# Both feed-forward blocks in two phases: all gate and up groups first, then the down projection as seven Strassen block types

## The chip, the cores and the metric

The kernel runs on one core of a Trainium2 chip. Its engines are TensorE (PE; the loading of its stationary operand has a row of its own, PEld), VectorE (DVE), ScalarE (ACT), GpSimd (POOL) and SyncE (SP, which only issues transfers here). Each engine works through its own list of instructions in order, and engines wait for each other by semaphores. The metric is the device time of one launch in microseconds, median over several runs.

## The reference

One decoder layer over 512 tokens of width 1024, in float32: a feed-forward block at half weight, a token mixer, a second feed-forward block at half weight, and a gated per-token embedding.

```python
def swiglu(x, w_gate, w_up, w_down):
    return (jax.nn.silu(x @ w_gate) * (x @ w_up)) @ w_down
...
h = h + 0.5 * swiglu(rmsnorm(h, ffn1_norm[i]), ffn1_w_gate[i], ffn1_w_up[i], ffn1_w_down[i])
n = rmsnorm(h, mix_norm[i])
proj = n @ w_in[i]
...
h = h + jnp.concatenate([ya, yb], axis=-1) @ w_out[i]
h = h + 0.5 * swiglu(rmsnorm(h, ffn2_norm[i]), ffn2_w_gate[i], ffn2_w_up[i], ffn2_w_down[i])
gate = jax.nn.sigmoid(rmsnorm(h, ple_norm[i]) @ ple_w_gate[i] + ple_b_gate[i])
h = h + gate * (p[i] @ ple_w_proj[i])
```

`w_gate` and `w_up` are 1024 x 2816 and `w_down` is 2816 x 1024, in each of the two feed-forward blocks (FFN1 and FFN2 below).

## The kernel before

**Products in three passes.** Every float32 operand is held as a rounded part and a remainder (`hi` and `lo`), and a product is the sum hi·hi + hi·lo + lo·hi on TensorE. A weight tile of 128 x 1024 (512 KB) is loaded (`raw`, `rawb`, `rawd`), cast by ACT into `whi` (L539), and the remainder is taken by DVE into `wlo` (L543). `whi` and `wlo` are rings of three buffers. So the cast for a step can begin only when the step three before it, the last reader of that buffer, has ended on PE. The down steps of the middle of an FFN have `whix` and `wlox`, one buffer each.

**Steps.** The program is a list of steps, each with its load, its cast and split, its product on PE, and work that follows the product (`after`, `post`). One function, `run`, writes all steps out in an order of its own: a step's product goes to PE, and around it the splits of the steps that come next and the `after` work of the steps before. Only `ENTRY`, a table written by hand, overrides that order for the first steps up to well into FFN2. PE, ACT, DVE and SP execute in that order word for word; POOL is ordered by the scheduler.

**Gate and up.** The 2816 features are 22 blocks of 128, taken in pairs: 11 groups per FFN. Group 0 is computed plainly. Groups 1 to 10 use Strassen's scheme in Winograd's form: seven products instead of eight for the 2 x 2 blocks (two halves of the features' rows by two halves of the tokens). Each product is one step of 24 matmuls over 256 columns (L756). They are run as 1, 7, 6, 4, 5, 2, 3. Products 6, 5 and 3 run in the same PSUM bank `a`, one on top of the other, and 4 in `mm`, so the values that stand between are read out on the way:

```python
def gate_sum(self, half):
    ps, kept = ((self.ps["q"], self.u2), (self.ps["a"], self.p7))[half]
    nc.vector.tensor_tensor(self.g[:, :, half], by_half(ps), by_half(kept), ALU.add)
```

`gate_sum(1)` (L896 with `a`) must have read the bank before product 3 writes it again. Around it stand, for each half of the tokens, the multiplication by the norm's factor (L901), the sigmoid on ACT (L903), a product with the factor (L907) and, at the end, the product with the up value (`finish`, L912).

**Down.** When a pair of groups is done, its gated product `g` is split (`ghi` by ACT, L923; `glo` by DVE, L925). Four steps then form its part of the down projection: 24 matmuls over 512 columns each (L255), of two of the eight row blocks of the output. They are not run at once: two of them are taken into each of the following groups.

```python
for i in (1, 7, 2, 6, 4, 5, 3) if j == 1 else (1, 7, 6, 4, 5, 2, 3):
    steps.append(gs[j][i])
    if i in ((5, 3 if at else 4) if j == 1 else (7, 5)):
        steps.append(here.pop(0))
```

So a group is 1, 7, down, 6, 4, 5, down, 2, 3. Each down step's result is added to the residual stream `h` by two DVE instructions (L959).

Of the kernel before, what the change touches and what calls it, by code (L numbers as in the profile page):

```python
# [39 lines left out]
G_6TS = (1, 2, 2, 2, 2, 2)  # L40
HT = T // 2
NP = ND // 2
# [13 lines left out]
product5 after4.1 split7 split7.1 load12 product6 split8:1 sums9 after5:1 split8 after6 after5:2  # L56
split9:2 split10.1:1 after5 product7 split10.1:1 split9 load14 product8 split10.1:1 after7
split10 split10.1 load15 product9 split11 after8 load16 product10 after9 split12 load17 after10
after10.1:1 product11 after11 split13 split14:1 after10.1 split14 product12 after+10 after11.1
after11.2 after12:1 product13 after+11 split15 after13:1 split16 after13:1 after12 product14  # L60
after13 ..after23 split26:1 after23:2 split26 after23 ..split101 after98:1 split101 after98
after+98 load104 product100 cast102 after+98 after99 rest100 split102 load105 split102 load105
product101 cast103 after+99 split103 rest101 load106 product102 cast104 after101 split104
rest102 load107 product103 cast105 after102 after102.1 split105 post102 load108 product104
cast106 after103 after103.1 after103.2 split106 post103 post103.1 load109 product105 cast107
after104 cast108 after104.1 after104.2 split107 split108 split107 post104 load110 product106
cast108 after105 ..product163 product163 split165:1 product163 after162 split165 load170
product164 split166 after163 after163.1 after164:1 product165 after164 product165 after+163
split167 after164 product166 after+164 split168:1 after165 split168 after165 after165.1
after165.2 product167 after+165 split169:1 after167:1 split169 after167:1 split169 after166:1  # L70
split170:1 sums171 split170 after166 split171:1 after166 load174 product168 after+166 split171:1
after+166 after167 split170 sums171 load175 product169 after168
# [11 lines left out]
)  # L84

PAD = {"sb": 96, "ffn_left": 256, "mix_left": 320, "ple_left": 256, "ffn_right": 96, "mix_right": 96, "ple_right": 0}
HEADS = 16
DT_AT = 112  # L90
# [22 lines left out]
def layer_kernel(ctx: ExitStack, tc: tile.TileContext, a: dict, out: bass.AP):  # L113
# [1720 lines left out]
    for side in region:  # L1834
        close_region(side)
# [100 lines left out]
```

## Time and profile before

| what | value |
|---|---|
| time, median of 3 runs | 1040.44 us (1040.24 to 1040.56) |
| profiled execution | 1040.32 us, span 1038.6 us |
| granted TensorE clock, mean | 0.997 |
| busy: PE, DVE, ACT, POOL | 99%, 75%, 50%, 13% of the span |
| matmuls | 6752 |
| DMA queue q1 (issued by SP) | 40304 packets, 128.86 MB, 36.1% of 16 engines' span |
| DMA queue q0 (issued by POOL) | 8640 packets, 31.46 MB, 17.7% |

The span is the time from the first to the last instruction; the profiled execution's own time lies 1.7 us above it. Busy shares are means over stages that differ, and a busy PE says that matmuls follow each other without a gap, not that they are short. The share of a DMA queue is the time that its packets took, as a share of 16 engines over the span. Rows of a timeline read: start in us, duration in us, engine, line, operation, output<-inputs, shapes, number; in brackets the idle time before it and who ended it.

### The profile page before, as it was taken

Reading aid. Unit: us, or ns where it says so; the run is one execution under the profiler, and the core shown is the slowest. Engines: PE = TensorE matmul, PEld = TensorE weight load, DVE = VectorE, ACT = ScalarE, POOL = GpSimd, SP = SyncE. Lnnn points to the kernel's source line nnn. Section 1 sums busy time; section 2 is a strip of 40 time slices with the busy share of each in tenths; the row PEclk is TensorE's granted clock in tenths of the full one; section 3 lists DMA queues with packets and bytes.
Section 4 is the critical chain, followed back from the end, with each engine's and each line's share of the span. In section 5 each row is a group of like instructions: output and inputs, shape, how many; then the busy total and the mean of one; then the engine's idle time right before and its main releaser. Section 6 shows DMA issues by size and latency. Waiting matters only on the chain.

```text
span 1038.6 us, 16733 instructions
## 1 busy us (share of the span) xinstructions
PE 1024.8 (99%) x6752; PEld 943.9 (91%) x6752; DVE 780.9 (75%) x1082; ACT 519.6 (50%) x716; POOL 135.6 (13%) x125
## 2 busy tenths in 40 slices
PE   8999999999999999999999999999999999999996
PEld 7999999999998899888888888899999999999886
DVE  6987776777677787776998757698777767676776
ACT  7754444434444474665854434454444444434554
POOL 0100000000000300044333000111000000000411
PEclk9999999999999999999999999999999999999998
DMA  9997767676623232544532323777767677634412
GB/s 338 320 234 206 204 185 185 167 198 177 145 61 122 71 114 94 158 149 123 159 103 64 119 83 122 223 183 207 206 162 192 160 191 195 191 103 130 135 42 81
DMA packets 50318, 163.55 MB, mean 157 GB/s; under 512 B 5696, under 2 KB 6208, under 8 KB 50240
## 3 DMA queue, kind: packets, MB, share of 16 engines
q1 hardware_dynamic: 40304, 128.86, 36.1%
q0 software_dynamic: 8640, 31.46, 17.7%
q10 hardware_dynamic: 1296, 2.16, 0.7%
q8 instruction: 53, 0.87, 0.3%
q14 instruction: 25, 0.20, 0.1%
HBM read 158.20 MB, written 4.26 MB: 156 GB/s over the span
## 4 chain that ended last, share of the span: by engine, by line
PE 86%; DVE 8%; ACT 2%; issue 2%; DMA 1%; SPq 0%; POOL 0%; DVEq 0%; ACTq 0%; POOLq 0%
PE sm L255 23%; PE mm L756 20%; PE a L756 15%; PE mm L241 6%; PE sm L241 5%; PE mm L255 4%; PE a L241 4%; PE a L255 3%; PE sm L842 1%; DVE wlo L543 1%; PE mm L842 1%; PE a L842 1%; DMA h<-in_x 1%; DVE tmp L1753 1%; PE sm L308 1%
## 5 line engine op out<-in xcount | busy, mean ns | idle before, releaser
L539 ACT CAST whi<-raw 128x1024 fp32r<-128x1024 f32 (+1 forms) x140 | 143.9, 1028 | 133.8 <-issue 42.6
L543 DVE TENSOR_TENSOR wlo<-raw,whi 128x1024 fp32r<-128x1024 f32 (+1 forms) x140 | 172.8, 1235 | 50.0 <-ACT whi L539 49.0
L756 PE MATMUL mm<-xfb,whi 128*128 128x256 f32 x960 | 163.8, 275 | 0.0
L756 PEld LDWEIGHTS mm<-xfb,whi 128*128 128x128 f32 x960 | 147.1, 192 | 1.0
L756 PE MATMUL mm<-xfb,wlo 128*128 128x256 f32 x480 | 132.3, 276 | 0.0
L255 PE MATMUL sm<-ghi,wlox 128*128 128x512 f32 x296 | 112.4, 380 | 0.5 <-DVE wlox L543 0.5
L255 PE MATMUL sm<-ghi,whix 128*128 128x512 f32 x296 | 112.4, 380 | 0.0
L255 PE MATMUL sm<-glo,whix 128*128 128x512 f32 x296 | 112.3, 380 | 0.0
L756 PE MATMUL a<-xfb,whi 128*128 128x256 f32 x640 | 109.2, 275 | 0.0
L756 PEld LDWEIGHTS a<-xfb,whi 128*128 128x128 f32 x640 | 98.7, 192 | 1.1
L756 PEld LDWEIGHTS mm<-xfb,wlo 128*128 128x128 f32 x480 | 92.3, 192 | 0.0
L756 PE MATMUL a<-xfb,wlo 128*128 128x256 f32 x320 | 88.2, 275 | 0.0
L543 DVE TENSOR_TENSOR wlox<-rawd,whix 128x1024 fp32r<-128x1024 f32 (+1 forms) x40 | 46.0, 1150 | 47.5 <-ACT whix L539 47.5
L903 ACT ACTIVATE g<-g 128x512 f32<-128x512 f32 x40 | 25.3, 632 | 106.6 <-DVE g L901 106.6
L543 DVE TENSOR_TENSOR wlo<-rawb,whi 128x1024 fp32r<-128x1024 f32 x52 | 63.6, 1223 | 17.8 <-ACT whi L539 17.7
L771 POOL DMA_DIRECT2D raw<-in_ffn_gu x20 | 17.6, 882 | 393.4 <-DVE h L959 138.1
L241 PE MATMUL sm<-x,whi 128*128 128x512 f32 x224 | 68.5, 388 | 0.0
L539 ACT CAST whi<-rawb 128x1024 fp32r<-128x1024 f32 x52 | 54.3, 1044 | 24.8 <-DVE rawb L766 18.9
L959 DVE SCALAR_TENSOR_TENSOR h<-sm,h 128x512 f32<-128x512 f32 x96 | 62.2, 685 | 3.1 <-PE sm L255 3.1
L255 PEld LDWEIGHTS sm<-ghi,wlox 128*128 128x128 f32 x296 | 56.1, 189 | 8.6 <-DVE wlox L543 0.9
L255 PEld LDWEIGHTS sm<-glo,whix 128*128 128x128 f32 x296 | 56.2, 190 | 6.8
L255 PEld LDWEIGHTS sm<-ghi,whix 128*128 128x128 f32 x296 | 56.2, 190 | 6.8
(388 smaller groups left out, 2394.5 us busy)
## 6 DMA issues: line engine op xcount, KB each, us to landing
raw<-in_ffn_gu SPq DMA_DIRECT2D x56, 512.0 KB, 6.4
rawd<-in_ffn_down SPq DMA_DIRECT2D x40, 512.0 KB, 4.2
rawb<-in_ffn_gu SPq DMA_DIRECT2D x32, 512.0 KB, 5.4
raw<-in_ffn_gu POOLq DMA_DIRECT2D x30, 512.0 KB, 5.7
raw<-in_w_in SPq DMA_DIRECT2D x28, 512.0 KB, 3.7
s<-in_ffn_gu SPq DMA_DIRECT2D x20, 512.0 KB, 7.3
s<-in_ffn_gu POOLq DMA_DIRECT2D x20, 512.0 KB, 8.6
raw<-in_w_out SPq DMA_DIRECT2D x16, 512.0 KB, 3.5
```

Source lines behind the costliest of these rows:

```text
L241: nc.tensor.matmul(ps, w, turned(x), start=first and n == 0, stop=last and n == 2, skip_group_check=True)
L255: nc.tensor.matmul(ps[:, tok], wt[:, c], turned(xt[:, tok]), start=first and k == i == 0, stop=last and k == len(xs) - 1 and i == len(by_p ...
L308: nc.tensor.matmul(ps[:, c : c + 1], part[:, c * P : (c + 1) * P], ones[:, 0:1], start=part is t, stop=part is not t or more is None,)
L539: nc.scalar.copy(self.hi[:, c], self.raw[:, c])
L543: nc.vector.tensor_tensor(self.lo[:, c], self.raw[:, c], self.hi[:, c].bitcast(F32), ALU.subtract)
L756: nc.tensor.matmul(o, wt[:, c], turned(xt), start=fresh and p == m == n == 0, stop=last and n == 2, skip_group_check=True,)
L771: nc.gpsimd.dma_start(w21.raw, self.src[0], accum_op=ALU.add)
L842: nc.tensor.matmul(ps, (whi, whi, wlo)[n][:, c], t[:, 0:2, n % 2].rearrange("p s (b i) -> p s i b", b=2), start=not lower and p == n == 0, ...
L903: nc.scalar.activation(t, t, AF.Silu)
L959: nc.vector.scalar_tensor_tensor(two(h[d]), back(ps[d]), 0.5, two(h[d]), ALU.mult, ALU.add)
L1753: engine.tensor_tensor(t, t, emb[d][:, tok], ALU.mult)
```

## The change

Each FFN becomes two phases. All ten Strassen groups run back to back; their gated products stay in one tile `G` of 128 x 2 x 2 x 10 x 256. Group 0's down projection follows as four plain steps of 12 matmuls over 512 columns. The down projection of the ten other groups is then one Strassen-Winograd product over 2 x 2 blocks: seven products, each of five steps of 24 matmuls over 256 columns, in the order 1, 7, 6, 4, 5, 2, 3.

```diff
+        steps = groups[0].plain_steps(at)
+        for j in range(1, NJ + 1):
+            steps += [gs[j][i] for i in ((1, 7, 2, 6, 4, 5, 3) if groups[j].turned else (1, 7, 6, 4, 5, 2, 3))]
+        steps += [down(i) for i in range(ND // 2)]
+        steps += blocks_down(a[f"{name}_dw"], shared, steps[-4:], out_norm, after, closed)
...
-            mine = groups[g0 - n : g0]
-            pending = [down(part, mine, i, each, last) for i in range(ND // each)]
-        steps += pending
```

The sums of weight blocks are formed by the DMA queue of POOL, which adds a block from memory to a tile that is already on chip. The sums of feature blocks are formed by DVE in `G` (`form`), and each of the seven feature operands is split in two parts by ACT and DVE (`split_form`) while the product before it runs. `ends` gives the work behind the last step of a product.

```diff
+            elif i in (4, 5, 2):
...
+                nc.sync.dma_start(raw, dw[{4: 3, 5: 2, 2: 1}[i], t])
+                if i == 5:
+                    nc.gpsimd.dma_start(raw, dw[3, t], accum_op=ALU.add)
...
+        def form(i, part):
...
+            nc.vector.scalar_tensor_tensor(to, one, -1.0, other, ALU.mult, ALU.subtract)
+
+        def split_form(i, part):
...
+            nc.scalar.copy(hi, g)
+            yield
+            nc.vector.tensor_tensor(lo, g, hi.bitcast(F32), ALU.subtract)
...
+        def q_done():
+            yield from add_to(2, 0, ps["q"], ALU.subtract)
+            yield from add_to(2, 0, kept["u2"], ALU.subtract, True)
+
+        ends = {
+            1: seeds, 7: lambda: keep("p7", "raw0", ps["q"]), 6: lambda: keep("u2", "g", ps["a"]),
+            4: q_done, 5: lower_done, 2: lambda: add_to(0, 0, ps["x"], ALU.add), 3: upper_done,
+        }
...
+            def split():
+                yield from w.split_by_engine(chain[t] if i in (1, 7, 6, 3) else kept[i, t])
+                if i in (1, 7, 6):
+                    yield
+                    nc.gpsimd.dma_start(chain[t], dw[{1: 2, 7: 3, 6: 1}[i], t], accum_op=ALU.add)
...
+            if i in (6, 4, 5):
+                also(at[0], "post", lambda i=i: form(i, parts[0]))
+                also(at[1], "post", lambda i=i: form(i, parts[1]))
+            also(at[0], "post", lambda i=i: split_form(i, parts[0]))
+            also(at[2], "post", lambda i=i: split_form(i, parts[1]))
```

```diff
-product5 after4.1 split7 split7.1 load12 product6 split8:1 sums9 after5:1 split8 after6 after5:2
+product5 after4.1 split7 split7.1 product6 split8:1 sums9 after5:1 split8 after6 after5:2
...
-+after166 after167 split170 sums171 load175 product169 after168
```

**What moves on DVE in a gate-and-up group.** Before, from the split for the down step behind product 5 to the additions of that step (line numbers of the kernel before; `wlo_1229` is the remainder for product 2, `wlo_1264` for product 3, `wlo_1296` for the next group's product 1, `g` the gated product):

```order
L543 TENSOR_TENSOR wlox_1199<-rawd_1029,whix_1198 128x1024
L543 TENSOR_TENSOR wlo_1229<-rawb_1067,whi_1228 128x1024
L896 TENSOR_TENSOR g_1232<-mm_1069,u_202_1196 128x2x256
L901 SCALAR_TENSOR_TENSOR g_1232<-g_1232,rall_497 128x2x256
L907 TENSOR_TENSOR g_1232<-g_1232,rall_497 128x2x256
L543 TENSOR_TENSOR wlo_1264<-rawb_843,whi_1263 128x1024
L896 TENSOR_TENSOR g_1232<-a_146_757,p_156_837 128x2x256
L901 SCALAR_TENSOR_TENSOR g_1232<-g_1232,rall_497 128x2x256
L907 TENSOR_TENSOR g_1232<-g_1232,rall_497 128x2x256
L543 TENSOR_TENSOR wlo_1296<-raw_196_1132,whi_1295 128x1024
L959 SCALAR_TENSOR_TENSOR h_96<-sm_1236,h_96 128x512
L959 SCALAR_TENSOR_TENSOR h_100<-sm_1249,h_100 128x512
```

Now the same place reads as follows (L519 is the remainder, L874 `gate_sum`, L879 and L885 the two multiplications, L890 `finish`; `wlo_1517` is for product 2, `wlo_1545` for product 3, `wlo_1577` and `wlo_1611` for the next group's products 1 and 7):

```order
L519 TENSOR_TENSOR wlo_1517<-rawb_1354,whi_1516 128x1024
L519 TENSOR_TENSOR wlo_1545<-rawb_1191,whi_1544 128x1024
L874 TENSOR_TENSOR G_629<-mm_1422,u_211_1514 128x2x256
L879 SCALAR_TENSOR_TENSOR G_629<-G_629,rall_488 128x2x256
L885 SCALAR_TENSOR_TENSOR G_629<-G_629,rall_488 128x2x256
L519 TENSOR_TENSOR wlo_1577<-raw_201_1420,whi_1576 128x1024
L874 TENSOR_TENSOR G_629<-a_197_1387,p_208_1484 128x2x256
L879 SCALAR_TENSOR_TENSOR G_629<-G_629,rall_488 128x2x256
L885 SCALAR_TENSOR_TENSOR G_629<-G_629,rall_488 128x2x256
L519 TENSOR_TENSOR wlo_1611<-raw_1452,whi_1610 128x1024
```

The chain of the gate now stands one remainder later: the one for product 3 is ahead of both sums, and the one for the next group's first product is between them.

**What moves on DVE in the down projection.** Before, a down step costs DVE the remainder of its weights, two additions to `h` and, once for four of them, the remainder of the gated product (the first rows of this piece, `glo`; the rows between belong to the next group):

```order
L543 TENSOR_TENSOR wlox_1058<-rawd_913,whix_1057 128x1024
L925 TENSOR_TENSOR glo_1062<-g_943,ghi_1061 128x1024
L766 TENSOR_TENSOR rawb_843<-rawb_843,s_163_878 128x1024
L543 TENSOR_TENSOR wlo_1096<-rawb_843,whi_1095 128x1024
L543 TENSOR_TENSOR wlo_1129<-raw_881,whi_1128 128x1024
L543 TENSOR_TENSOR wlo_1159<-s_163_878,whi_1158 128x1024
L959 SCALAR_TENSOR_TENSOR h_95<-sm_1100,h_95 128x512
L959 SCALAR_TENSOR_TENSOR h_99<-sm_1113,h_99 128x512
```

Now, between the splits for product 4's last steps and those for product 5's third (L994 is `form`, L1004 the remainder of a feature operand `xfb`, L1028 and L1026 are `q_done`; `wlo_3433` belongs to product 4's last step, `wlo_3465`, `wlo_3494` and `wlo_3528` to product 5's first three):

```order
L519 TENSOR_TENSOR wlo_3433<-xfa_3048,whi_3432 128x1024
L994 SCALAR_TENSOR_TENSOR G_629<-G_629 128x1024
L1004 TENSOR_TENSOR xfb_3437<-G_629,xfb_3437 128x1024
L519 TENSOR_TENSOR wlo_3465<-xfa_3113,whi_3464 128x1024
L994 SCALAR_TENSOR_TENSOR G_629<-G_629 128x1536
L519 TENSOR_TENSOR wlo_3494<-xfa_3113,whi_3493 128x1024
L1004 TENSOR_TENSOR xfb_3437<-G_629,xfb_3437 128x1536
L1028 TENSOR_TENSOR h_96<-h_96,sm_3015 128x2x256
L1028 TENSOR_TENSOR h_97<-h_97,sm_3016 128x2x256
L1026 TENSOR_TENSOR h_96<-h_96,g_3370 128x2x256
L1026 TENSOR_TENSOR h_97<-h_97,g_3370 128x2x256
L519 TENSOR_TENSOR wlo_3528<-raw_3179,whi_3527 128x1024
```

Forms, remainders of features and the additions of the product before stand in one queue with the remainders of the weights.

**What moves on PE at the end of FFN1.** Before, the norm's sums (L308, with `ssum` from POOL) stand behind two whole units of the mixer (the end of the second):

```order
L241 MATMUL mm_3669<-x_3656,whi_3600 128x512
L241 MATMUL mm_3669<-x_3657,whi_3600 128x512
L241 MATMUL mm_3669<-x_3656,wlo_3601 128x512
L308 MATMUL sm_3704<-ones_77,ssum_3551 128x1 [waits PE_49,Pool_49]
L308 MATMUL sm_3704<-ones_77,ssum_3551 128x1 x3
L241 MATMUL sm_3711<-x_3512,whi_3647 128x512 [waits PE_49]
```

Now they stand (L284) behind three halves of 12 matmuls, and ahead of the third unit:

```order
L217 MATMUL mm_3988<-x_4018,whi_3945 128x512 [waits Activation_49]
L217 MATMUL mm_3988<-x_4019,whi_3945 128x512 [waits DVE_49]
L217 MATMUL mm_3988<-x_4018,wlo_3946 128x512
L284 MATMUL sm_4066<-ones_76,ssum_3809 128x1 [waits Pool_49]
L284 MATMUL sm_4066<-ones_76,ssum_3809 128x1 x3
L217 MATMUL sm_4073<-x_3801,whi_4001 128x512
```

The wait for POOL has moved up by 12 matmuls over 512 columns.

353 lines of the change are left out of this document (217 added, 136 removed).

## The prediction

> **What bounds the kernel now.** I read the page's first lines, then the chain that ended last inside one gate-and-up group of FFN1, then what DVE and ACT did in that group, then the DMA queues.
>
> ```profile
> span 1038.6 us, 16733 instructions
> PE 1024.8 (99%) x6752; PEld 943.9 (91%) x6752; DVE 780.9 (75%) x1082; ACT 519.6 (50%) x716; POOL 135.6 (13%) x125
> ...
> q1 hardware_dynamic: 40304, 128.86, 36.1%
> q0 software_dynamic: 8640, 31.46, 17.7%
> ```
>
> PE is without work for 13.8 us of the span (1038.6 - 1024.8). So the kernel gains only from fewer or shorter matmuls, and loses whatever time another engine makes PE wait. In the chain, each line is one step: start, length, bank, line, matmuls.
>
> ```profile
> 185.06 2.68 PE a L756 x24
> 187.74 2.68 PE mm L756 x24
> 190.42 2.68 PE a L756 x24
> 193.10 5.18 PE sm L255 x24
> 198.28 2.68 PE mm L756 x24
> 200.96 2.68 PE a L756 x24
> 203.64 2.46 PE mm L756 x22
> ```
>
> These are product 6, 4, 5, a down step, 2, 3 and the next group's 1. Each begins where the one before ends. A step of 24 matmuls over 256 columns takes 2.68 us, one over 512 takes 5.18.
>
> DVE in the same stretch, with the remainder for product 2, `gate_sum(0)`, its two multiplications, the remainder for product 3, `gate_sum(1)`:
>
> ```profile
> 190.54 1.22 DVE L543 TENSOR_TENSOR wlo<-rawb,whi 128x1024 fp32r<-128x1024 f32 x1
> 191.67 0.69 DVE L896 TENSOR_TENSOR g<-mm,u 128x512 f32<-128x512 f32 x1
> 192.39 0.69 DVE L901 SCALAR_TENSOR_TENSOR g<-g,rall 128x512 f32<-128x512 f32 x1
> 193.78 0.69 DVE L907 TENSOR_TENSOR g<-g,rall 128x512 f32<-128x512 f32 x1 [0.69 <-ACT g L903]
> 194.72 1.22 DVE L543 TENSOR_TENSOR wlo<-raw,whi 128x1024 fp32r<-128x1024 f32 x1 [0.25 <-ACT whi L539]
> 195.86 0.68 DVE L896 TENSOR_TENSOR g<-a,p 128x512 f32<-128x512 f32 x1
> ```
>
> From the start of the first remainder to the end of `gate_sum(1)` it is 196.54 - 190.54 = 6.00 us. `gate_sum(1)` reads bank `a`, which product 3 writes from 200.96: there are 4.42 us to spare. They are there because a down step of 5.18 us stands between.
>
> **The change, part by part.** *Fewer matmul columns.* Per FFN 20 down steps of 5.18 us (103.6) become 35 of 2.68 (93.8); group 0's four steps stay. That is -9.8 us per FFN, -19.6 in all. The gate and up products do not change in number.
>
> *The gate's chain without its cover.* `whi` has three buffers, so the cast for product 3 waits until product 4 has ended, which is when product 5 starts; call that moment zero. That the ring binds like this stands in one row of ACT: a cast beginning as the step at 198.28 ends (200.96).
>
> ```profile
> 200.93 1.05 ACT L539 CAST whi<-raw 128x1024 fp32r<-128x1024 f32 x1 [2.05 <-issue]
> ```
>
> In the new order the remainder for product 3 stands ahead of `gate_sum(0)`, so the same six DVE instructions as in the rows above, with the remainders one step later, begin at 1.05 and `gate_sum(1)` ends at 1.05 + 6.00 = 7.05. Product 3 is due after products 5 and 2, at 5.36. PE waits 1.7 us. Behind it the queue has room: two multiplications and the sigmoid between them end near 9.3, the next group's second remainder at 10.5, due at 12.4. So it is one wait of 1.7 per group, each group anew. Check from the other side: 4.42 to spare, less the 5.18 removed, less some 1.0 that the first remainder starts later: -1.8. Nine groups of an FFN at 1.7, and the last at about 0.9, since the next step's remainder has 512 columns instead of 1024: 16.2 per FFN, +32.4 in all. Bounds: 0 if something lets the cast start a step earlier, 2.4 per group if the semaphores between the three engines add more than in the rows.
>
> *DVE in the block products.* Durations, the page's first two rows of DVE, then the groups kept apart by shape, then one sum of two weight blocks from the timeline:
>
> ```profile
> L543 DVE TENSOR_TENSOR wlo<-raw,whi 128x1024 fp32r<-128x1024 f32 (+1 forms) x140 | 172.8, 1235 | 50.0 <-ACT whi L539 49.0
> ...
> L959 DVE SCALAR_TENSOR_TENSOR h<-sm,h 128x512 f32<-128x512 f32 x96 | 62.2, 685 | 3.1 <-PE sm L255 3.1
> ```
>
> ```profile
> L925 DVE TENSOR_TENSOR glo<-g,ghi 128x1024 fp32r<-128x1024 f32 x20 | 27.4, 1372 | 21.9 <-ACT ghi L923 21.9
> L923 ACT CAST ghi<-g 128x1024 fp32r<-128x1024 f32 x20 | 27.3, 1364 | 46.1 <-DVE g L912 44.6 <-DVE g L874 1.5
> ```
>
> ```profile
> 208.24 1.24 DVE L766 TENSOR_TENSOR rawb<-rawb,s 128x1024 f32<-128x1024 f32 x1
> ```
>
> From the remainder for product 4's third step to that for product 5's third, DVE has five weight remainders (6.17), two forms (1.24, and 1.86 for the one with 1536 columns, scaled), two feature remainders (1.37 and 2.06, scaled) and the four additions of `q_done` (2.74): 15.4. It also waits for ACT's copy behind each form: 1.36, and 2.05 less the remainder that stands between, 0.8. That makes 17.6. Neighbours in the rows overlap by 0.09 (190.54 + 1.22 against 191.67); for eleven that is -1.0, so 16.6. PE does five steps in 13.4. It waits 3.2 us. Products 6 and 4 have forms but not these additions: 16.6 - 2.4 = 14.2, 0.8 each. Products 1 and 3 have additions, and 3 the mixer's operands, in place of forms: I take 0.8 each, as for those with forms; products 7 and 2 fit. 6.4 per FFN, +12.8 in all. Bounds: 0 (if the queue has run ahead) and 20.
>
> *The hand-over to the mixer and to the last gate.* The last product ends only `h`'s upper row blocks. Behind it come two additions, the squares on ACT and four sums on POOL, and PE asks for them after three halves of 12 matmuls, 3 x 2.59 = 7.8 us.
>
> ```profile
> 338.28 6.48 POOL L298 TENSOR_TENSOR ssum<-ssum,tmp 128x512 f32<-128x512 f32 x4 [5.75 <-ACT tmp L297]
> ```
>
> Four sums take 6.5 us; with one addition and the operands and squares on ACT ahead of them (some 3.5 us) that is 10.0, a wait of 2.2. Twice: +4.4, bounds 0 and 6. The order written by hand ends early now, and the start of FFN2 and of the mixer run in `run`'s own: I take +3, with 0 and 8 as bounds (8 is over half of all the time that PE was idle before).
>
> *Transfers.* Nothing is added to PE's path if they keep ahead. The loads of q1 take 36.1% of 1038.6 us for 128.86 MB, 1.53 us for 512 KB; those of q0 17.7% for 60 of 512 KB, 3.06 us each. A group has five of the one and three of the other: 16.8 us, of a period of 18.8 + 1.7. The down phase has 20 plain ones and 20 that add: 91.8 us, of 93.8 + 10.4 + 6.4 = 110.6 us. That fits, but POOL issues the adding ones in one queue, behind tiles that must come free first: +2, bounds 0 and 16.
>
> *Without cost:* the gains of 0.5 ride on instructions that were there; ACT is at 50%; `L894` is one DVE instruction of 0.69 in every second group and runs after `gate_sum(1)`.
>
> The sum: -19.6 + 32.4 + 12.8 + 4.4 + 3 + 2 = +35.0 on the profiled 1040.32, 1075.3. That execution is 0.12 us below the median, so I give 1075.
>
> **A rule beside it.** One group of before, with its down steps, reads: length, then busy time of PE, PEld, DVE, ACT, POOL, and the granted clock.
>
> ```profile
> 185.10:214.20 29.10, 29.10 (x218) 27.83 (x217) 20.92 (x24) 12.91 (x15) 2.54 (x3) 1.00 0.69 178
> ```
>
> DVE is busy 72% of it. Without two down remainders, four additions and `glo` 14.3 us are left of 18.8, 76%; in the block products it is 12.7 of 13.4 (five remainders, forms and feature remainders), 95%. The Trainium skill ("Perfetto Trace Analysis", Optimization Strategy) says that where the most contended engine changes between regimes of a kernel, interleaving them may help. It gives no figure; spread evenly, DVE's work would fit under PE's, and the sum would be the -19.6 alone. By that rule the change, which takes the two regimes apart, gives up cover, and these rows agree.
>
> **The rivals.** *The waits stay hidden, and it is faster.* For it speaks that no row of before shows PE waiting in a group; against it, the order of DVE and the ring. It decides at `gate_sum(1)` ending before 5.36; below 0.6 us of wait per group and none in the block products the change gains. Then 1040.4 - 19.6 + 3 = 1024.
>
> *Only the gate's wait is real.* DVE may run ahead in the down phase, since the steps of 5 us are gone and nothing else is queued. 1040.4 - 19.6 + 32.4 = 1053.
>
> *Transfers become the bound.* A group at present has the DMA engines busy for 0.69 of its time, without waiting. If adding transfers can't be had at more than 0.69 of 16 engines, the down phase takes 91.8 / 0.69 = 133 us in place of 110.6 and a group 24.3 in place of 20.5; half of that, since loads run ahead into the plain steps, is 11 + 19 per FFN, over 1100; with the down phase alone, 1075 + 22 = 1097.
>
> *The clock drops.* It is 1.00 in the row above and lower only at the end, where PE is idle:
>
> ```profile
> 1030.00:1038.60 8.60, 1.11 (x8) 0.87 (x8) 3.26 (x10) 2.16 (x4) 0.00 (x0) 0.69 0.57 213
> ```
>
> My longest wait is 3.2 us, twice. If it halved the clock for some 4 us afterwards, that would be +2 each, 1079. The Trainium skill ("TensorE: Matmul & The Clock Gate", HAM oscillation) warns of idle gaps above about 3.4 us; no row of before has such a gap between matmuls.
>
> **How the numbers follow.** Both waits, as summed: 0.65, from 1060 to 1090. Only the gate's wait: 0.12. Transfers: 0.09. The clock: 0.02. Hidden waits and a gain: 0.09. Within the 0.2% that a measurement can tell here: 0.03, where parts of each cancel. The point is the likeliest case's, 1075. The range leaves out the gain, the draw, and the worst of the transfers: 1050 to 1094. Faster 0.09, same 0.03, slower 0.88.
>
> **What would show it.** In the profile after: matmuls 7472 in place of 6752; a step of product 3 in every group starting about 1.7 us behind the end of product 2, with DVE's sum of `a` as the releaser; in the down phase one gap of about 3 us at product 5's third step; the sums of POOL as a wait of some 2 us behind both FFNs; the clock at 1.00. Gaps released by DMA would mean the third rival. I'm wrong if the group's period is 18.8 us: then the chain of DVE started earlier than the ring allows by my reading.

## The result: 1137 us, 9% slower, and the profile after

The changed kernel takes 1137.25 us (1135.79 to 1139.86, 4 runs), 1.0935 times the kernel before (interval 1.0915 to 1.0956). The forecast was 1075, with a range up to 1094: the sign was right, the size was not. The profiled execution took 1137.24 us. Its page, in the lines that answer to those of before, then the mean granted clock:

```profile
span 1135.5 us, 18390 instructions
PE 1039.8 (92%) x7472; PEld 973.3 (86%) x7472; DVE 827.8 (73%) x1084; ACT 576.9 (51%) x764; POOL 169.4 (15%) x165
```

```profile
core 0: 1135.5 us, clock 0.976
```

Two things stand in the page's second line. PE is without work for 95.7 us (1135.5 - 1039.8), where it was 13.8 before: 81.9 more. And PE is busy 15.0 us longer, though its work by 2.68 and 5.18 us a step is 19.6 us shorter: its matmuls took 34.6 us longer than that. Most of it is the clock: its mean fell from 0.997 to 0.976, which is 24 us of such a span.

Where it went, by stage. Of before, then of after: FFN1 from the first product of group 1, the mixer, FFN2, the last gate (length, busy PE, PEld, DVE, ACT, POOL, granted clock, DMA share, GB/s).

```profile
39.10:341.70 302.60, 302.10 (x2209) 287.57 (x2208) 226.77 (x259) 143.43 (x174) 28.52 (x31) 1.00 0.65 175
341.70:653.90 312.20, 311.95 (x1755) 273.59 (x1754) 243.77 (x399) 167.92 (x272) 58.14 (x40) 1.00 0.36 112
653.90:979.70 325.80, 324.83 (x2318) 307.31 (x2317) 241.13 (x290) 150.61 (x184) 33.49 (x35) 1.00 0.66 179
979.70:1038.60 58.90, 50.13 (x323) 45.25 (x321) 38.55 (x82) 30.02 (x47) 12.39 (x11) 0.95 0.19 65
```

```profile
39.40:387.00 347.60, 309.17 (x2569) 302.54 (x2568) 249.23 (x259) 169.48 (x194) 45.26 (x51) 0.97 0.71 181
387.00:706.20 319.20, 315.15 (x1756) 275.35 (x1755) 244.19 (x400) 170.32 (x276) 61.15 (x42) 0.99 0.38 118
706.20:1073.40 367.20, 328.16 (x2678) 319.08 (x2677) 263.11 (x289) 177.04 (x203) 45.83 (x51) 0.98 0.69 175
1073.40:1135.50 62.10, 51.46 (x324) 46.52 (x322) 40.51 (x85) 32.70 (x51) 14.12 (x12) 0.94 0.30 102
```

FFN1 is 45.0 us longer, FFN2 41.4, the mixer 7.0, the last gate 3.2, the start 0.3. In FFN1 the gate and up groups and the down projection part here:

```profile
39.40:264.30 224.90, 199.44 (x1682) 197.41 (x1680) 153.04 (x171) 101.49 (x127) 23.87 (x28) 0.95 0.69 178
264.30:387.00 122.70, 109.72 (x890) 105.12 (x889) 96.18 (x89) 67.99 (x68) 21.39 (x23) 0.99 0.74 188
```

The 70 products of the groups should take 70 x 2.68 = 187.6 and took 224.9: 37.3 more. The down projection should take 10.4 + 93.8 = 104.2 and took 122.7: 18.5 more. FFN2 loses 35.2 and 17.8. The waits of PE, in the list of the trace: engine, bank and line that wait, who was waited for, us in all, times, the longest.

```profile
PE a L731 <- DVE G L874: 47.4, 19, 4.6
PE a L1091 <- DVE wlo L519: 14.2, 10, 2.9
PE sm L231 <- DVE h L930: 8.5, 6, 1.6
```

Half of the idle time stands in the first line: product 3 waits for `gate_sum(1)` (L874), as forecast, but not evenly. In FFN1 every second group looks as forecast. DVE, with the remainder for product 3 and the two sums, and PE's first matmul of product 3:

```profile
119.42 1.23 DVE L519 TENSOR_TENSOR wlo<-raw,whi 128x1024 fp32r<-128x1024 f32 x1 [0.80 <-ACT whi L515]
120.56 0.68 DVE L874 TENSOR_TENSOR G<-mm,u 128x512 f32<-128x512 f32 x1
...
124.75 0.68 DVE L874 TENSOR_TENSOR G<-a,p 128x512 f32<-128x512 f32 x1
```

```profile
125.58 0.46 PE L731 MATMUL a<-xfb,whi 128*128 128x256 f32 x2 [1.80 <-DVE G L874]
```

Moment zero, product 5's first matmul, is 118.25; the remainder starts at 1.17, `gate_sum(1)` ends at 7.18 and product 3 starts at 7.33: due at 5.36, it is 1.97 late. (The timeline shows 1.80, since the modelled end of the last matmul lies 0.17 behind the next step's due start. Waits below are as the timeline shows them.) In the group behind it, POOL, ACT and PE:

```profile
127.06 0.84 POOL L746 DMA_DIRECT2D raw<-in_ffn_gu  x1 [15.76 <-DMA raw<-in_ffn_gu]
128.81 0.86 POOL L749 DMA_DIRECT2D s<-in_ffn_gu  x1 [0.91 <-DMA s<-in_ffn_gu]
133.54 0.85 POOL L783 DMA_DIRECT2D rawb<-in_ffn_gu  x1 [3.87 <-DVE wlo L519]
```

```profile
141.34 1.05 ACT L515 CAST whi<-rawb 128x1024 fp32r<-128x1024 f32 x1 [3.18 <-DMA rawb<-in_ffn_gu]
```

```profile
148.57 0.64 PE L731 MATMUL a<-xfb,whi 128*128 128x256 f32 x2 [3.99 <-DVE G L874]
```

L783 is the adding transfer that forms product 3's weights. POOL issues it behind the two sums for the next group (L746, L749); it lands 7.8 us after its issue, and the cast starts at 141.34 where moment zero was 139.05. Those 2.3 us pass down the whole chain: 3.99 in place of 1.80. And behind the long wait the matmuls are slow. The 24 matmuls of product 3 after 1.80 us of wait, after 3.99, and after the 2.27 at 103.15:

```profile
125.58:128.40 2.82, 2.82 (x25) 2.82 (x26) 1.85 (x3) 1.60 (x2) 0.84 (x1) 1.00 0.37 145
148.57:152.90 4.33, 4.33 (x24) 4.33 (x25) 3.39 (x4) 1.56 (x2) 0.00 (x0) 0.61 0.94 183
103.15:107.50 4.35, 4.35 (x25) 4.35 (x26) 3.41 (x4) 1.57 (x2) 0.85 (x1) 0.64 0.96 159
```

So the late transfer costs such a group 2.2 us of wait and 1.5 of clock.

In the down projection, the forecast wait at product 5's third step is there: DVE's four additions of `q_done` and the remainder, then PE, with 2.88 us where 3.2 was forecast. Not forecast were waits in group 0's plain steps: PE stands until DVE has emptied the bank `sm` into `h` (the first PE row below).

```profile
342.90 1.26 DVE L1028 TENSOR_TENSOR h<-h,sm 128x512 f32<-128x512 f32 x2
344.09 1.27 DVE L1026 TENSOR_TENSOR h<-h,g 128x512 f32<-128x512 f32 x2
345.30 3.48 DVE L519 TENSOR_TENSOR wlo<-raw,whi 128x1024 fp32r<-128x1024 f32 x3
```

```profile
274.80 0.67 PE L231 MATMUL sm<-xfa,whi 128*128 128x512 f32 x2 [1.58 <-DVE h L930]
...
346.56 0.49 PE L1091 MATMUL a<-xfb,wlo 128*128 128x256 f32 x1 [2.88 <-DVE wlo L519]
```

At the hand-over to the mixer PE waits 3.81 us for four sums of POOL that took 7.44 (forecast 2.2, for 6.5):

```profile
391.28 7.44 POOL L274 TENSOR_TENSOR ssum<-ssum,tmp 128x512 f32<-128x512 f32 x4 [10.64 <-ACT tmp L273]
```

### The profile page after: what moved, and what is told of

It reads as the page before. It is cut to its first block, busy times and chain, and to the rows that moved or that the text cites. A ratio compares the mean times of both kernels' runs of the same rounds, so it can differ in the third digit from the quotient of the medians.

```text
span 1135.5 us, 18390 instructions
## 1 busy us (share of the span) xinstructions
PE 1039.8 (92%) x7472; PEld 973.3 (86%) x7472; DVE 827.8 (73%) x1084; ACT 576.9 (51%) x764; POOL 169.4 (15%) x165
## 5 line engine op out<-in xcount | busy, mean ns | idle before, releaser
L519 DVE TENSOR_TENSOR wlo<-raw,whi 128x1024 fp32r<-128x1024 f32 (+3 forms) x162 | 195.3, 1208 | 58.6 <-ACT whi L515 58.5
L515 ACT CAST whi<-raw 128x1024 fp32r<-128x1024 f32 (+3 forms) x162 | 163.2, 1011 | 135.7 <-PE a L217 24.0
L731 PE MATMUL a<-xfb,whi 128*128 128x256 f32 x640 | 126.2, 301 | 49.8 <-DVE G L874 47.4
L731 PEld LDWEIGHTS a<-xfb,whi 128*128 128x128 f32 x640 | 109.3, 214 | 53.0 <-issue 50.5
L519 DVE TENSOR_TENSOR wlo<-rawb,whi 128x1024 fp32r<-128x1024 f32 x76 | 93.5, 1231 | 71.2 <-ACT whi L515 70.9
L731 PE MATMUL a<-xfb,wlo 128*128 128x256 f32 x320 | 95.3, 298 | 0.8 <-DVE wlo L519 0.8
L1091 PE MATMUL a<-xfb,whi 128*128 128x256 f32 x480 | 84.1, 280 | 1.3 <-ACT whi L515 1.2
L1091 PE MATMUL a<-xfb,wlo 128*128 128x256 f32 x240 | 68.1, 284 | 14.2 <-DVE wlo L519 14.2
L1091 PEld LDWEIGHTS a<-xfb,whi 128*128 128x128 f32 x480 | 74.2, 195 | 2.7 <-ACT whi L515 2.2
L519 DVE TENSOR_TENSOR wlo<-s,whi 128x1024 fp32r<-128x1024 f32 x36 | 45.8, 1282 | 33.1 <-ACT whi L515 32.9
L731 PEld LDWEIGHTS a<-xfb,wlo 128*128 128x128 f32 x320 | 68.7, 215 | 1.0 <-DVE wlo L519 1.0
L746 POOL DMA_DIRECT2D raw<-in_ffn_gu x20 | 17.3, 864 | 338.2 <-DMA raw<-in_ffn_gu 115.3
L1002 ACT CAST xfb<-G 128x1024 fp32r<-128x1024 f32 (+1 forms) x28 | 46.0, 1641 | 29.8 <-DVE G L994 29.8
L1091 PEld LDWEIGHTS a<-xfb,wlo 128*128 128x128 f32 x240 | 46.7, 195 | 16.2 <-DVE wlo L519 16.1
L1004 DVE TENSOR_TENSOR xfb<-G,xfb 128x1024 fp32r<-128x1024 f32 (+1 forms) x28 | 46.4, 1656 | 18.0 <-ACT xfb L1002 17.9
```

What stands on the lines that cost most here:

```text
L515: nc.scalar.copy(self.hi[:, c], self.raw[:, c])
L519: nc.vector.tensor_tensor(self.lo[:, c], self.raw[:, c], self.hi[:, c].bitcast(F32), ALU.subtract)
L731: nc.tensor.matmul(o, wt[:, c], turned(xt), start=fresh and p == m == n == 0, stop=last and n == 2, skip_group_check=True,)
L746: nc.gpsimd.dma_start(w21.raw, self.src[0], accum_op=ALU.add)
L1002: nc.scalar.copy(hi, g)
L1004: nc.vector.tensor_tensor(lo, g, hi.bitcast(F32), ALU.subtract)
```

## The experiments

The theory after the comparison: (A) the cover of the down steps is gone, which costs 1.97 us per group; (B) the late sum for product 3 adds to that in every second group; (C) waits of about 2 us and more lower the clock behind them; (D) the order that `run` writes causes most of the down projection's loss. Rivals: transfers as such are the bound, or DVE's total work is. Ratios are to the kernel before.

### 1. The gate's chain first

```diff
-... split, after, i in (1, 7, 6, 3))
+... split, after, i in (1, 7, 6, 4, 5, 3))
```

The last argument says that the `after` work of the step goes ahead of the next splits.

> The kernel after, with products 4 and 5 of a gate-and-up group marked urgent, so that their gate sums stand ahead of the next remainder on DVE; not an instruction more or less. Theory A (place of the gate chain behind product 3's remainder, whose cast waits for a weight sum that lands late in every second group, and the clock loss that long waits bring): the waits ahead of product 3, 2.0 us in one group and 2.4 to 4.7 in the next, fall to 0.2 to 0.5 in all, the slow product 3 behind them goes, 1137 becomes 1065 to 1085. Rival B (the DMA engines are full in this phase): the transfers are the same, so the period of a group of about 22 us stays and the time is above 1120.

Measured: 1123.69 us, 1.0802 (1.0784 to 1.082). The gain is 13.6 us, well short of the 52 to 72 expected. The waits for the gate's sum are 21.8 us where they were 47.4, and the even groups wait some 0.4 us; the odd ones still wait, because now the late remainder stands in DVE's queue ahead of the second multiplication and `gate_sum(1)`:

```profile
97.55 0.69 DVE L879 SCALAR_TENSOR_TENSOR G<-G,rall 128x512 f32<-128x512 f32 x1
100.75 1.23 DVE L519 TENSOR_TENSOR wlo<-rawb,whi 128x1024 fp32r<-128x1024 f32 x1 [2.51 <-ACT whi L515]
101.89 0.69 DVE L885 SCALAR_TENSOR_TENSOR G<-G,rall 128x512 f32<-128x512 f32 x1
102.49 0.69 DVE L874 TENSOR_TENSOR G<-a,p 128x512 f32<-128x512 f32 x1
```

An in-order queue passes a late transfer on to whatever stands behind it. That pointed at (B) as a cause of its own.

### 2. Without the late sum

```diff
-                if i == 6:
-                    yield
-                    nc.gpsimd.dma_start(w11.raw, self.src[1], accum_op=ALU.add)
```

> The kernel after, without the adding transfer that forms product 3's weights behind product 6 (product 3 multiplies product 6's weights; one of eight 512 KB transfers of a group is left out). Theory A: the groups with 2.4 to 4.7 us come down to the 2.0 of the others and no product 3 runs slow, -17 us per FFN: 1100 to 1108. Rival B (full DMA engines): a gain of an eighth or more in every group alike, also in those with 2.0. A third one (the clock alone makes the difference between the groups): nothing changes, 1130 to 1138.

Measured: 1107.40 us, 1.0643 (1.0628 to 1.0659), 29.9 us less than the changed kernel. The list of waits has product 3's as follows (L871 is `gate_sum`):

```profile
PE a L731 <- DVE G L871: 34.2, 20, 2.6
```

34.2 in 20 waits is 1.71 each; PE is busy 1027.4 us in place of 1039.8. So (B) and what follows it in the clock are 29.9 us, and (A) is left at about 2 us per group. The groups alone gain more: those of both FFNs, by the profiles, take 415.3 us (38.95 to 246.03 and 711.60 to 919.85) where the changed kernel takes 447.7, so 32.4 of their 72.5 us of loss go and 40.1 stay.

### 3. The cover taken away in the kernel before

The second down step of groups 4 to 9 of FFN1 stands behind product 3 instead of behind product 5; nothing else differs.

```diff
-if i in ((5, 3 if at else 4) if j == 1 else (7, 5)):
+if i in ((5, 3 if at else 4) if j == 1 else (7, 3) if name == "ffn1" and 4 <= j <= 9 else (7, 5)):
```

> The kernel before, with the second down step of groups 4 to 9 of FFN1 taken from behind product 5 to behind product 3; the same steps. Theory A: without a step between product 5 and product 2, these six groups each wait 1.9 us or more ahead of product 3, and those whose weight sum is late 2.4 or more with a slow product behind: +11 to +25 us, 1052 to 1065. Rival C (the down steps protect by lending DVE and DMA time to the group as a whole, wherever they stand): within 3 us of 1040.

Measured: 1053.13 us, 1.012 (1.0104 to 1.0135), 12.6 us more than before.

```profile
PE a L756 <- DVE g L896: 10.8, 6, 1.8
```

Six waits of 1.80, as in the changed kernel, and 2.1 us of time for each. The work of every engine is the same as before: it is the place of the down step that hid the chain, and (A) is shown. No sum is late here, though POOL's order is as in the changed kernel.

### 4. Group 0's down steps

Experiment 1, and the additions of the plain down steps ahead of the next splits.

```diff
-                lambda: w.split_by_engine(), (add,),
+                lambda: w.split_by_engine(), (add,), True,
```

> As e1_gate_first, and group 0's four down steps marked urgent as well, so that their additions to h stand ahead of the next remainder on DVE. Theory A: the waits of 0.7 to 1.6 us of those steps for a PSUM bank, 5.0 us per FFN, fall to under 2: 7 to 10 us less than e1_gate_first. If instead they come from the late weights of these steps, the two are the same within 2 us.

Measured: 1121.27 us (1113.95 to 1125.2), 1.0766 (1.0725 to 1.0808). The waits for `h` fall from 11.7 to 2.8 us, but the times of the two kernels overlap: by time alone this is inconclusive.

### 5. Product 3 behind the next group's product 1

```diff
+            if j > 2:
+                at3 = steps.index(gs[j - 1][3])
+                steps[at3], steps[at3 + 1] = steps[at3 + 1], steps[at3]
```

> The kernel after, with product 3 of groups 2 to 9 run behind the next group's product 1 instead of ahead of it: the same instructions, and one step of 2.68 us more between product 5 and product 3. Theory A (gate sum of bank a and the late weight sum are both due at product 3, at 5.36 us, and ready at 7.2 and later): due at 8.04, both are met in time, the waits of eight groups in each FFN and their slow products go, about 28 to 32 us per FFN: 1137 becomes 1072 to 1085. Rival B (transfers fill the phase): under 15 us gained. Rival D (only the place moves: product 3 waits less, but the next group's first products wait instead, since DVE's queue is the bound): 20 to 40 us gained, with waits at product 7 or 6.

Measured: 1113.98 us, 1.0705 (1.0687 to 1.0723). The even groups wait no more; the odd ones that were moved still wait 2.06 to 2.81 us in FFN1 and 1.06 to 2.53 in FFN2, since the sum now lands later too. POOL, then ACT:

```profile
129.71 0.86 POOL L749 DMA_DIRECT2D s<-in_ffn_gu  x1 [1.01 <-DMA s<-in_ffn_gu]
130.25 1.18 POOL L783 DMA_DIRECT2D rawb<-in_ffn_gu  x1
```

```profile
143.22 1.04 ACT L515 CAST whi<-rawb 128x1024 fp32r<-128x1024 f32 x1 [3.58 <-DMA rawb<-in_ffn_gu]
```

It was issued right behind two others and took 13.0 us to the cast. More time for the chain does not help when the transfer's place in the queue sets its end.

### 6. The same, and the down projection's additions in a better order

Experiment 5 with the edit of experiment 4, and `q_done` and `lower_done` behind the next splits.

```diff
-            s = Step(product, ..., (ends[i],) if last else (), last)
+            s = Step(product, ..., (ends[i],) if last else (), last and i not in (4, 5))
```

> As e5_third_later, and two places in the down phase: group 0's four plain steps urgent (additions to h ahead of the next remainder on DVE), and the additions behind products 4 and 5 not urgent (behind the next remainder). Expected against e5_third_later: the plain steps lose some 4 us of their 5.6 per FFN, as e1 and e4 showed in waits (11.7 against 2.8 us for both FFNs); product 5's third step waits about 0.5 us in place of 2.9, with the slow matmuls behind it gone: 10 to 16 us less in all, 1058 to 1072. If product 5's wait is one for the adding transfers, it stays and only the plain steps gain.

Measured: 1101.81 us, 1.0599 (1.0583 to 1.0615), 12.2 us less than experiment 5. The difference is as expected, the time is not, since the odd groups still waited. In the profiled executions 9.2 us of the difference lie in the down projections (245.0 to 235.8 us for both), 6.7 of them in the plain steps. So (D) is shown for about 9 of the 36.3 us that they lose.

### 7. More matmuls

Product 2's 24 matmuls are issued twice in each group: 480 more, 53.6 us of PE's time by 2.68 each.

```diff
                 self.product(i, to, fresh)
+                if i == 2:
+                    self.product(i, to, fresh)
```

> The kernel after, with the 24 matmuls of product 2 issued twice in every Strassen group (the up value of one half of the tokens counts that product twice): 480 matmuls, 53.6 us of PE work more. Theory A with the clock (the waits ahead of product 3 are idle time, and those of 2.4 us and more also slow the matmuls behind them): the filler falls into the waits, the slow products go; 1125 to 1140, no slower than without it. Theory A without a cost of the clock: +4 to +10 us, 1141 to 1148. Rival (PE or its feed is the bound in this phase): +54 us, 1190.

Measured: 1128.72 us, 1.084 (1.0812 to 1.0868): 8.5 us faster than the changed kernel, with 480 more matmuls.

```profile
PE a L731 <- DVE G L876: 4.9, 7, 1.2
```

The waits for the gate's sum go from 47.4 to 4.9 us. By the clock, 0.987 of 1126.0 in place of 0.976 of 1135.5, some 12.6 us more come back. A group is bound by the length of its chain, not by PE's work. This run alone doesn't speak against DVE, whose work is what it was (828.2 us); experiment 14 does, where the same work takes 87.6 us less.

### 8. POOL in the program's order

POOL is added to the engines whose instructions the scheduler may not reorder; L783 then stands ahead of the next group's two sums.

```diff
     ORDERED = {
-        mybir.EngineType.PE, mybir.EngineType.Activation, mybir.EngineType.DVE, mybir.EngineType.SP
+        mybir.EngineType.PE, mybir.EngineType.Activation, mybir.EngineType.DVE, mybir.EngineType.SP, mybir.EngineType.Pool
     }
```

> The kernel after, with POOL's instructions in the order in which the program names them, as the other four engines have it: the adding transfer for product 3's weights then stands ahead of the two for the next group, not behind them. Theory A' (in every second group that transfer lands late because POOL's queue serves the next group's two sums first): all waits ahead of product 3 become 2.0 us and the slow products go, as without the transfer: 1100 to 1112. Rival (it lands late because the DMA engines are full, in whatever order): within 8 us of 1137.

Measured: 1111.05 us (1105.98 to 1115.95), 1.0682 (1.0636 to 1.0728), 26.2 us less. POOL at the same group:

```profile
128.23 0.84 POOL L783 DMA_DIRECT2D rawb<-in_ffn_gu  x1 [19.18 <-DVE wlo L519]
128.77 1.19 POOL L746 DMA_DIRECT2D raw<-in_ffn_gu  x1
129.30 1.53 POOL L749 DMA_DIRECT2D s<-in_ffn_gu  x1
```

All transfers are there, and most of what experiment 2 gained by leaving one out is gained by its place in the queue: 26.2 of 29.9 us in the time, 23.9 of 32.4 in the groups. Transfers as such are not the bound of the groups.

### 9 and 10. Both orders, then sums asked for earlier

Experiment 9 is experiment 6 with the edit of 8.

> e6_later_and_order with POOL in program order. Theory A': the 2.0 to 2.8 us that every second group still waits ahead of product 3 there (19.2 us in the waits, and some 6 us of slow matmuls) go, since the sum now lands before its new due time: 1068 to 1082. Rival as above: 1095 or more.

Measured: 1074.77 us, 1.0327 (1.03 to 1.0355), 27.0 us less than experiment 6. Product 3's waits for the sum are 6.2 us in 4. With the cover back and the sum in time, (A) and (B) are nearly gone. Experiment 10 asks for the weight sums a step earlier, and for the norm's sums 12 matmuls later:

```diff
-                    do(i + 3, "sums")
...
+            do(i + 4, "sums")
...
-    behind_product(2, mix_steps[1].late, mix_steps[2].late)
+    behind_product(2, lambda: mix.update(ps=mix_norm.sums()), mix_steps[1].late, mix_steps[2].late)
```

> e9_order_all, with the sum of product 6's weights one step earlier on DVE, and the norm's sums for the mixer asked for by PE 12 matmuls (2.6 us) later. Expected: the 0.4 and 0.6 us that a group waits at products 7 and 6 (about 1 us in 16 groups) go or halve, and the 3.8 us behind FFN1 become 1.2, with its slow matmuls: 8 to 18 us less than e9_order_all. If the sum's own weights are not there a step earlier, nothing is gained in the groups.

Measured: 1060.84 us, 1.0202 (1.0175 to 1.0229), 13.9 us less than experiment 9.

### 11. Sums on POOL instead of adding transfers

For product 5's weights in the down projection; besides, product 2's additions stand behind the next splits, and the mixer's operands are formed a step later.

```diff
-                    nc.gpsimd.dma_start(raw, dw[3, t], accum_op=ALU.add)
+                    nc.gpsimd.tensor_tensor(raw, raw, kept[4, t], ALU.add)
...
-            s = Step(product, ..., last and i not in (4, 5))
+            s = Step(product, ..., last and i not in (2, 4, 5))
...
-        also(made[2][3], "post", lambda: lower_parts((4, 5)))
-        also(made[2][4], "post", lambda: lower_parts((6, 7)))
+        also(made[2][4], "post", lambda: lower_parts((4, 5)))
+        also(made[3][0], "post", lambda: lower_parts((6, 7)))
```

> e10_sums_earlier, with three edits in the down phase: product 5's weight sums by a POOL addition of product 4's tiles, which are still on chip, in place of ten adding transfers of 512 KB; the mixer's lower operands one step later on DVE; product 2's additions to h behind the next remainder. In e10 a transfer of product 5 takes 15.4 us from issue to landing and PE waits 2.7 and 0.7 us for it, with slow matmuls behind, in FFN1, with the DMA engines at 1.06 of their time. If the DMA engines' time is the bound there: these waits go in both FFNs, and product 3's 1.0 and 1.6 us fall below 0.6: 8 to 18 us less, 1043 to 1053. If it is only the order of POOL's queue: the waits stay within 1 us and only the 4 us of product 3 go, 1055 to 1060. The bound that would then remain is DVE's.

Measured: 1068.62 us, 1.027 (1.0252 to 1.0287): 7.8 us slower than experiment 10. POOL's addition, and DVE's remainder beside it:

```profile
294.09 2.67 POOL L987 TENSOR_TENSOR raw<-raw,raw 128x1024 f32<-128x1024 f32 x1 [14.32 <-DMA raw<-in_ffn_dw]
```

```profile
294.49 3.36 DVE L519 TENSOR_TENSOR wlo<-raw,whi 128x1024 fp32r<-128x1024 f32 x1
```

The remainder takes 3.36 us where it takes 1.23 elsewhere, and DVE's busy time grows from 823.7 us in experiment 10 to 840.8, with ten such additions. The two other edits hardly cost the time: experiment 12 has them as well and is 5.3 us faster than 10. The Trainium skill ("SBUF — State Buffer", Who interferes with whom) says that a VectorE instruction with two inputs in SBUF contends with a GpSimd instruction that reads SBUF; this trace agrees, and puts 2.1 us on it.

### 12 to 14. What holds product 5 back

Experiment 12 keeps the adding transfers, with the two moves of 11, product 3 of one more group run later, and a shorter lead for product 2's loads:

```diff
-            if j > 2:
+            if j > (2 if at else 1):
...
-            s.lead = 12
+            s.lead = 5 if i == 2 else 12
```

> e10_sums_earlier (adding transfers for product 5 as there), with the loads of product 2's weights asked for seven steps later, so that they no longer run beside product 5's sums; product 2's additions and the mixer's lower operands one place later on DVE, as in e11; and the later product 3 for the first two groups of FFN2 as well. If product 5's wait in e10 comes from transfers that crowd the same 15 us: it falls from 2.7 and 0.7 us to under 1 us in FFN1, with the slow matmuls behind it, and product 3's waits halve: 10 to 16 us less than e10, 1045 to 1052. If DVE alone had been the bound there, only the 3 to 6 us of the other edits come: 1054 to 1058.

Measured: 1055.56 us (1054.92 to 1060.28), 1.0155 (1.0135 to 1.0176). The loads stood where they were (296.6 us, 295.6 without the edit), so it says nothing on them. In FFN1's down projection product 5 still waited 2.7 us for a cast, and ACT for a transfer (6.1 us, the longest of its waits there):

```profile
PE a L1094 <- ACT whi L515: 2.7, 1, 2.7
```

In the next two, product 3's five adding transfers of the down projection are left out (13), or issued five steps later, behind product 5's (14):

```diff
-                if i in (1, 7, 6):
+                if i in (1, 7):
```

```diff
-                if i in (1, 7, 6):
+                if i in (1, 7, 4):
...
-                    nc.gpsimd.dma_start(chain[t], dw[{1: 2, 7: 3, 6: 1}[i], t], accum_op=ALU.add)
+                    nc.gpsimd.dma_start(chain[t], dw[{1: 2, 7: 3, 4: 1}[i], t], accum_op=ALU.add)
```

> e12_loads_apart without the adding transfers that form product 3's weights in the down phase (product 3 multiplies product 6's weights; 10 of 40 adding or plain transfers of 512 KB in a down phase of FFN1 and FFN2 together are left out). If product 5's third step waits for its sum because these transfers stand between: its 2.7 and 0.8 us and the slow matmuls behind fall under 0.6: 4 to 8 us less than e12. If product 5's sums are late by themselves (their loads wait for buffers): no change within 2 us.

> e12_loads_apart with the same adding transfers for product 3 issued five steps later, behind product 5's sums in POOL's queue. If their place between product 5's sums makes the wait: as e13, 1048 to 1052, with nothing left out. If it is the total that the DMA engines carry in those 15 us: about half of e13's gain. If product 5's sums are late by themselves: 1054 to 1057.

Measured: 1051.91 us (1049.09 to 1055.49), 1.0122 (1.0102 to 1.0142), and 1049.66 us (1049.11 to 1050.35), 1.0089 (1.0074 to 1.0104). Against experiment 12 that is 3.7 and 5.9 us less; the runs of 13 scatter over more than the difference between the two. Moving the transfers gives what leaving them out gives: their place ahead of product 5's sums was the cause of that wait, which is gone in experiment 14. Its page (the waits for the gate's sum are 1.9 us in two):

```profile
PE 1013.1 (97%) x7472; PEld 950.6 (91%) x7472; DVE 824.3 (79%) x1084; ACT 575.1 (55%) x764; POOL 172.0 (16%) x165
```

It does the whole work of the change, in another order, 87.6 us faster than the changed kernel (idle 34.3 us in place of 95.7, PE busy 26.7 us less, clock 0.998). It is still 9.2 us behind the kernel before. The 19.6 us of shorter products are eaten by 20.5 us more of idle time than before (34.3 - 13.8) and 7.9 us of PE's busy time over 1024.8 - 19.6; much of the latter may be the 0.17 that each wait adds to the modelled end, which no run separates. A version below the kernel before was not found.

## Why the prediction was wrong, point by point

| term of the sum | forecast | measured |
|---|---|---|
| gate and up groups, both FFNs | +32.4 | +72.5 (37.3 + 35.2) |
| of it: the chain without its cover | +32.4 | +40.1: what the groups still lose in experiment 2 |
| of it: the late sum, with its clock | within +2 | +32.4: what experiment 2 takes off the groups (29.9 off the whole time) |
| down projection, both FFNs | +12.8 | +36.3 (18.5 + 17.8) |
| hand-over and order | +7.4 | +10.5 (mixer, last gate, start) |

With the -19.6 these make 99.7; 2.8 of it the kernel before lost in the same stages itself, which leaves the 96.9 by which the span grew.

- **The gate's chain** was right in mechanism and place, and a fifth short in size: 1.97 us late in the group shown where 1.7 was forecast, and 40.1 us in all for 32.4. Experiments 3, 5 and 7 show it from three sides: take the cover away from the kernel before and the wait appears; give some back and it goes.
- **The step that failed is the one on transfers**: "Nothing is added to PE's path if they keep ahead", "+2, bounds 0 and 16". What it put at 2 cost about 30 us: one late transfer in most of the odd groups (experiment 2). The step compared busy time of the DMA engines with a period, and named POOL's single queue without following it. The right comparison was of one transfer: from DVE's release of its tile, through the queue, to the cast. The order of POOL could be read before; how long a transfer takes behind two others had to be bounded. That order alone isn't enough: the kernel before has it too (L771, L774 and L808 at 203.72, 204.98 and 212.17 us), without a late sum, and so has experiment 3. What differs is the length of a group, 29.1 us there and some 22 here. After, the row of DMA issues shows the ten sums of the odd groups, eight of them late, with their median time to land (512 KB each):

```profile
rawb<-in_ffn_gu POOLq DMA_DIRECT2D x10, 512.0 KB, 7.6
```

Moment zero came 5.5 us after the issue (139.05 - 133.54). In experiment 8, where this sum stands first, the same row has 5.6. The sign that the prediction named, gaps released by DMA, would have missed this: no wait of PE is put down to a DMA, since the cast, the remainder and `gate_sum(1)` stand between.

- **The clock rival** got 0.02 and +2 per wait of 3.2 us. The mean says 27 us in all (0.024 of 1135.5). The clock fell behind the 2.27 above, and in experiment 8 behind a wait of 1.91; but behind 2.60 in FFN2 it stayed at 1.00, and so it did behind 2.91 at 1034.54. Each wait and the 24 matmuls behind it, of experiment 8, then of the changed kernel:

```profile
224.41 0.46 PE L731 MATMUL a<-xfb,whi 128*128 128x256 f32 x2 [1.91 <-DVE G L874]
...
224.41:228.80 4.39, 4.39 (x25) 4.39 (x26) 3.45 (x4) 1.57 (x2) 0.00 (x0) 0.61 0.00 0
```

```profile
747.83 0.46 PE L731 MATMUL a<-xfb,whi 128*128 128x256 f32 x2 [2.60 <-DVE G L874]
...
747.50:750.50 3.00, 2.67 (x24) 2.70 (x25) 2.00 (x4) 1.59 (x2) 1.71 (x2) 1.00 0.47 53
```

Behind the 1.80 of the changed kernel's even groups it never fell. The Trainium skill ("TensorE: Matmul & The Clock Gate", Part 1: The HAM clock gate) has the clock at half after an idle window of about 3.4 us, in windows that run free. Free-running windows would let the same wait cost something in one place and nothing in another, as here, though no run shows that this is the reason; that a wait must reach 3.4 us is not borne out.
- **The down projection**: product 5's wait was right (2.88 for 3.2). Product 6 waits 0.76 and 0.77 and product 4 0.50, where 0.8 each was forecast, and product 1 doesn't wait in FFN1. Not seen were the plain steps, which lose about 5.0 us per FFN: they were costed at no wait, though their additions stand behind the splits of the steps to come. Product 3's first steps wait 1.0 and 1.6 where 0.8 was taken. In FFN1 these waits make 12.5 of the 18.5 us; some 0.17 for each of ten and the clock of 0.63 for 4.64 us behind the 2.88 are part of the rest. Experiments 6 and 14 show that order, of the additions and of the transfers, not DVE's work, causes most of it: in experiment 14 the down projections take 223.9 us where the changed kernel takes 244.7, with DVE's busy time at 824.3 us and 827.8.
- **The hand-over**: 3.81 and 1.59 us in place of 2.2 twice; behind both the clock falls, to 0.50 from 398.77 to 404.00 us and from 1084.60 to 1086.00.
- **The rivals**: "Transfers become the bound" gave 1097 with the down phase alone; with the groups its own terms (11 + 19 us per FFN) come to 1135, next to the measured 1137. That is luck, not its mechanism: the DMA engines ran at 0.74 in the down projection, where this rival capped them at 0.69; experiment 8 moves the same bytes 26 us faster. "Waits stay hidden" is refuted by experiment 3.
- **What would show it**: 7472 matmuls, product 3's lateness, the wait at product 5's third step and the waits for POOL's sums were there; the clock at 1.00 was not.

## What to carry to other kernels

When steps are taken out from between others, list every chain that had the removed step as its slack, and then follow each transfer on those chains through its issuing queue, one by one: a share of the DMA engines says nothing about one that stands behind two others. Waits add up worse than their sum, since those of about 2 us and more can also slow the matmuls behind them; on one critical chain, filler work can be faster than waiting. Where a kernel's order was written around its steps, price the new order before the arithmetic saved.

## What the runs showed of the hardware

- The granted clock fell behind single waits ahead of product 3 as short as 1.91 us by the timeline (24 matmuls in 4.39 us in place of 2.82, clock 0.61), and at the hand-over to the last gate behind 1.59 us with eight one-column matmuls after it. It stayed at 1.00 behind others of 2.60 and 2.91. 480 more matmuls made a kernel 8.5 us faster.
- An adding transfer of 512 KB landed 7.6 us after its issue (median of ten in the changed kernel) when two stood ahead of it in POOL's queue, and 5.6 us after it when it stood first (experiment 8). Issued right behind two others, it took 13.0 us to its reader's start (experiment 5).
- POOL's addition of two 128x1024 tiles (2.67 us) stretched a VectorE subtraction of that shape from 1.23 to 3.36 us.
